# Sending the first three stores of a softmax kernel from a second queue while its loads run

## The chip, the cores and the metric

One NeuronCore of a Trainium2 chip (trn2) runs the whole kernel. The metric is the device time of one execution in microseconds (us), lower is better.

## The reference

```python
def reference(x):                      # x: 16 x 1024 x 512, float32
    x_scaled = x / 2.0
    x_max = np.max(x_scaled, axis=-1, keepdims=True)
    exp_x = np.exp(x_scaled - x_max)
    return (exp_x / np.sum(exp_x, axis=-1, keepdims=True)).astype(np.float32)
```

33.55 MB come in and 33.55 MB go out. Seen by the 128 partitions of on-chip memory there are 128 "rows" of 512 numbers per partition; one row over all partitions is 256 KB.

## The kernel before

Nine tiles of 3, 5, 9, 15, 21, 31, 15, 17 and 12 rows share one arena of 99 rows. Tiles 7 and 8 reuse the space of tiles 0 to 2 and of tile 3, so their loads wait for those tiles' stores. Compute goes by chunks of 3 to 8 rows: VectorE takes the negated maximum, ScalarE the exponentials with their sums, VectorE (two chunks later) the reciprocal and the multiply, in place.

All loads and stores are issued by SyncE on one queue, in a fixed order:

```python
PLAN = [   # per tile: rows of each chunk, first arena row
    ([3], 0), ([5], 3), ([5, 4], 8), ([5] * 3, 17), ([7] * 3, 32), ([8, 8, 8, 7], 53),
    ([5] * 3, 84), ([6, 6, 5], 0), ([4] * 3, 17),
]
QUEUE = [
    ("load", 0), ("load", 1), ("load", 2), ("load", 3), ("load", 4), ("load", 5),
    ("load", 6), ("store", 0), ("store", 1), ("store", 2), ("store", 3), ("load", 7),
    ("store", 4), ("load", 8), ("store", 5), ("store", 6), ("store", 7), ("store", 8),
]
# ... cut ...
    def do_queue(items):
        for kind, t, *rest in items:
            # ... cut ...
            if kind == "load":
                for u in behind.get(t, []):          # tiles whose space this one takes
                    nc.sync.wait_ge(st[u], stored[u])
                # ... nc.sync.dma_start(...).then_inc(ld[t], 16)
                continue
            nc.sync.wait_ge(s_mul, k + 1)            # k: last chunk of the tile
            # ... nc.sync.dma_start(...)
# ... cut ...
        for k in range(len(chunks) + LAG):           # VectorE, LAG = 2
            if k < len(chunks):
                do_max(k)
            if k >= LAG:
                do_mul(k - LAG)
```

The softmax here doesn't subtract the row's maximum and nothing guards it: scores larger than these inputs give would overflow.

## Time and profile before

| | |
|---|---|
| time, median of the first 3 runs | 163.24 us (162.96 to 163.44) |
| span of the profiled run | 161.1 us |
| VectorE busy | 125.1 us (78%) |
| ScalarE busy | 94.0 us (58%) |
| DMA packets' time, share of 16 DMA engines | 97.8% |

A row of digits on the page is the span in 40 slices of about 4 us, each digit the busy share in tenths. A queue line gives packets, MB, and the packets' time as a share of the span of all 16 DMA engines. A line of DMA issues gives the size in KB and the us from issue to landing. "SPq" is SyncE's sequencer, "ACTq" ScalarE's. In the list of waits the numbers are us in total, times, and the longest.

### The profile page before, as it was taken

The numbers are of one execution on the slowest core, as the hardware profiler recorded it, in microseconds if no ns is written. First come the engines' busy times: TensorE is split into PE (matmuls) and PEld (weight loads), VectorE is DVE, ScalarE is ACT, GpSimd is POOL, SyncE is SP. The second block draws the span as 40 slices with busy tenths as digits, with TensorE's granted clock in tenths as the row PEclk, the third lists the DMA queues.
The fourth block names the chain that finished last, engine by engine and source line by source line (L and its number), as shares of the span: only waits on it lengthen the run. The fifth ranks groups of instructions, "written<-read, shape, count | busy, mean of one in ns | idle before, by whom it ended". The sixth has DMA issues, their size and how long they took to land.

```text
span 161.1 us, 494 instructions
## 1 busy us (share of the span) xinstructions
DVE 125.1 (78%) x174; ACT 94.0 (58%) x257; POOL 0.2 (0%) x4
## 2 busy tenths in 40 slices
DVE  0557989999999999999999999999999994000000
ACT  3455957674977949696977764697875770000000
POOL 0000000000000000000000000000000000000000
DMA  7999999997996998999999989899899979999991
GB/s 264 458 476 397 458 404 480 450 490 331 504 473 286 458 397 292 458 433 458 419 413 458 480 382 491 363 416 552 349 457 489 426 340 458 409 439 415 420 464 61
DMA packets 2595, 67.13 MB, mean 417 GB/s; under 512 B 288, under 2 KB 288, under 8 KB 544
## 3 DMA queue, kind: packets, MB, share of 16 engines
q1 hardware_dynamic: 2592, 67.11, 97.8%
q14 instruction: 3, 0.02, 0.0%
HBM read 33.55 MB, written 33.55 MB: 416 GB/s over the span
## 4 chain that ended last, share of the span: by engine, by line
DVE 69%; DMA 13%; issue 0%; DVEq 0%; SPq 0%
DVE negmax L115 38%; DVE arena L128 30%; DMA arena<-in_x_dram 13%; DVE recip L124 1%; DVEq L209 0%; SPq L100 0%
## 5 line engine op out<-in xcount | busy, mean ns | idle before, releaser
L141 ACT ACTIVATE arena<-arena,negmax 128x512 f32<-128x512 f32 x128 | 90.7, 709 | 37.1 <-DVE negmax L115 37.1
L115 DVE TENSOR_REDUCE negmax<-arena 128x5 f32<-128x2560 f32 (+5 forms) x23 | 71.7, 3116 | 9.0 <-DMA arena<-in_x_dram 9.0
L128 DVE TENSOR_SCALAR arena<-arena,recip 128x512 f32<-128x512 f32 x128 | 52.8, 482 | 0.8
L141 ACT ACTIVATION_READ_ACCUMULATOR arena<-arena,negmax 128x1 f32 x128 | 23.9, 187 | 0.0
L124 DVE RECIPROCAL recip<-sums 128x5 f32<-128x5 f32 (+5 forms) x23 | 4.2, 181 | 0.0
L141 ACT ACT_TABLE_LOAD x1 | 1.3, 1283 | 1.3 <-PEq L198 1.3
L198 POOL MEMSET const-bfloat16-1.0<- 128x1 bf16 x1 | 0.1, 101 | 0.0
L198 POOL MEMSET const-uint8-127<- 128x1 uint8 x1 | 0.1, 101 | 0.0
L198 POOL MEMSET const-float32-0.0<- 128x1 f32 x1 | 0.1, 98 | 0.2 <-issue 0.2
L198 POOL MEMSET const-float32-1.0<- 128x1 f32 x1 | 0.1, 98 | 0.0
## 6 DMA issues: line engine op xcount, KB each, us to landing
arena<-in_x_dram SPq DMA_DIRECT2D x1, 7936.0 KB, 50.9
out_dram<-arena SPq DMA_DIRECT2D x1, 7936.0 KB, 36.5
arena<-in_x_dram SPq DMA_DIRECT2D x2, 3840.0 KB, 40.8
out_dram<-arena SPq DMA_DIRECT2D x2, 3840.0 KB, 32.5
arena<-in_x_dram SPq DMA_DIRECT2D x1, 5376.0 KB, 32.4
out_dram<-arena SPq DMA_DIRECT2D x1, 5376.0 KB, 32.0
arena<-in_x_dram SPq DMA_DIRECT2D x1, 4352.0 KB, 19.7
out_dram<-arena SPq DMA_DIRECT2D x1, 4352.0 KB, 25.5
```

The costliest lines, as they stand in the source:

```text
L115: nc.vector.reduce_max(out=negmax[:, b : b + c], in_=arena[:, a : a + c], axis=mybir.AxisListType.X, negate=True,)._wait_ge(ld[t], loads_o ...
L124: nc.vector.reciprocal(out=recip[:, b : b + c], in_=sums[:, b : b + c])._wait_ge(s_exp, k + 1).then_inc(s_rec, 1)
L128: ins = nc.vector.tensor_scalar_mul(out=arena[:, a + r], in0=arena[:, a + r], scalar1=recip[:, b + r : b + r + 1],)
L141: ins = nc.scalar.activation(out=arena[:, a + r], in_=arena[:, a + r], func=mybir.ActivationFunctionType.Exp, bias=negmax[:, b + r : b + r ...
L198: nc = _bacc.Bacc("TRN2", target_bir_lowering=False, num_devices=1)
```

## The change

In the kernel before, the stores of tiles 0 to 2 are ready at 17 to 32 us, but stand behind seven loads and land at 66 to 75 us. The change issues these 17 rows from ScalarE's own queue as soon as they are ready, so that they leave while the loads run and the space for tile 7 comes free early. The core of the diff:

```diff
 QUEUE = [
     ("load", 0), ("load", 1), ("load", 2), ("load", 3), ("load", 4), ("load", 5),
-    ("load", 6), ("store", 0), ("store", 1), ("store", 2), ("store", 3), ("load", 7),
+    ("load", 6), ("store", 3), ("load", 7),
     ("store", 4), ("load", 8), ("store", 5), ("store", 6), ("store", 7), ("store", 8),
 ]
+SIDE = {2: 0, 3: 1, 5: 2}          # after the exponentials of chunk k: store this tile
@@ the store part of do_queue becomes a function of the engine @@
+    def do_store(engine, t, lo, hi, groups):
+        ...
+        engine.wait_ge(s_mul, k + 1)
+        ... engine.dma_start(...)
@@ ScalarE's loop over the chunks @@
             ins.then_inc(s_exp, 1)
+            if k in SIDE:
+                do_store(nc.scalar, SIDE[k], 0, tiles[SIDE[k]][1], [(0, P, 1)])
```

## The prediction

> **What bounds the kernel now**
>
> I read the busy rows first, then the DMA part, then the chain, then the stores one by one. The page's busy rows and its queue line:
>
> ```profile
> DVE  0557989999999999999999999999999994000000
> ACT  3455957674977949696977764697875770000000
> DMA  7999999997996998999999989899899979999991
> ...
> q1 hardware_dynamic: 2592, 67.11, 97.8%
> ```
>
> Each digit is a fortieth of the span, about 4 us. VectorE has six empty slices at the end, ScalarE too; the DMA row is full from the second slice to the last but one, and the one queue's packets fill 97.8% of the 16 DMA engines' time. So the span is that of moving 67.11 MB, and 2.2% of 161.1 us, 3.5 us, is all that better packing of the same packets could ever give back. The stretches say what the ends cost:
>
> ```profile
> 0.00:2.00 2.00, 0.00 (x0) 0.74 (x1) 0.20 (x4) 1.00 0.49 117
> 60.00:64.00 4.00, 4.00 (x8) 4.00 (x12) 0.00 (x0) 1.00 0.80 250
> 66.00:84.00 18.00, 17.89 (x27) 13.82 (x39) 0.00 (x0) 1.00 1.03 444
> 158.00:161.00 3.00, 0.00 (x0) 0.00 (x0) 0.00 (x0) 1.00 0.06 25
> ```
>
> The last two columns are the DMA share and GB/s (a packet is booked where it starts, so short windows scatter around 1.00). The fill costs 1.0 us (half of 2), the closing stretch 1 to 2, and one dip at 60 to 64 us about 1.4. The change adds no byte and touches none of the three.
>
> The chain of waits would mislead here:
>
> ```profile
> DVE 69%; DMA 13%; issue 0%; DVEq 0%; SPq 0%
> ```
>
> It ends with VectorE's last multiply at 134.86 us; the 25 us of stores after that are not in it.[...]
>
> The queue in order of time, from SyncE's timeline in narrow windows (start, issue time), and the two ends of the DMA list (KB, us to landing):
>
> ```profile
> 17.31 0.35 SPq L108 DMA_DIRECT2D out_dram<-arena  x1
> 21.70 0.34 SPq L108 DMA_DIRECT2D out_dram<-arena  x1
> 31.76 0.33 SPq L108 DMA_DIRECT2D out_dram<-arena  x1
> ...
> 127.31 0.33 SPq L108 DMA_DIRECT2D out_dram<-arena  x1
> 134.89 0.33 SPq L108 DMA_DIRECT2D out_dram<-arena  x1
> ```
>
> ```profile
> out_dram<-arena SPq DMA_DIRECT2D x1, 2304.0 KB, 43.1
> out_dram<-arena SPq DMA_DIRECT2D x1, 1280.0 KB, 47.7
> out_dram<-arena SPq DMA_DIRECT2D x1, 768.0 KB, 49.0
> ```
>
> The stores of tiles 0, 1 and 2 (3, 5 and 9 rows per partition) are issued at 17.3, 21.7 and 31.8 us but land at 66.3, 69.4 and 74.9: they stand behind the seven loads issued in the first 3.9 us. That is the wait which the change removes. But the DMA engines are not idle meanwhile; they move the loads.
>
> **Rates.** The fifth load (21 rows) lands at 34.8 us and the sixth (31 rows) at 53.8: 19.0/31 = 0.613 us per row of 256 KB. The store of tile 3 (15 rows) lands at 83.95, after the one before at 74.9: 9.05/15 = 0.603 us. Loads alone and stores alone run at one rate, 428 to 435 GB/s. The 256 rows moved (128 in, 128 out) at 0.607 are 155.4 us; with 1.0 of fill, 1.4 of dip and 2 to 3 of ending that is the span.
>
> **What the Trainium skill says**
>
> "DMA: Bandwidth & Descriptors", section "Issuing engines are not separate DMA queues": transfers begun by ScalarE, SyncE or GpSimd run on the same 16 DMA engines and interleave; a second issuer saves only sequencer time. The trace of before has one queue and cannot test that; but it shows that sequencer time is not short (0.33 us per issue, 18 issues).
>
> The same page, section "Queues, rings and completion order": each DMA engine takes turns between the queue rows that have work, a packet at a time. The profile counts 2592 packets, 18 transfers of 144, and 288 of them under 512 B: so 128 data packets and 16 small ones per transfer, one data packet per partition, as long as the tile's rows (6 KB for 3 rows, 62 KB for 31). If turns are taken by these packets, a short store gets a small share beside a long load. No trace here shows it yet.
>
> The same page, section "Where 436 GB/s comes from": 435.2 GB/s for the ports of one core. The trace agrees in size: 428 to 435 on long transfers, 417 over the span. So there is no faster rate to go to, unless a load and a store in one DMA engine overlap.
>
> **The change, part by part**
>
> Removed from SyncE: three waits and three issues, 3 x 0.34 us, beside nothing that is short of time. Worth 0.
>
> Added on ScalarE: after the exponentials of chunks 2, 3 and 5, a wait and an issue of about 0.35 us (up to 0.8, as the longest on SyncE). The waits are for the multiplies of chunks 0, 1 and 3, done at 17.3, 21.7 and 31.7 us; the three exponential groups end at 19.5, 22.4 and 33.6. So ScalarE waits little or not at all. In ScalarE's timeline it then idles for the next maximum: 2.59 us before the exponential at 25.03 and 0.89 before that at 34.49. The second and third issues fall into this, and the first pushes the next five exponentials by 0.4 us, which the 2.59 swallow. On the path: 0.
>
> Moved: 17 rows of store, 17 x 0.61 = 10.4 us of DMA time, from after the seventh load to between the loads. The loads after it land later by at most 10.4 us. What that does on VectorE: the fourth load is used as it lands (a 0.50 us wait before the maximum at 22.18); the fifth lands at 34.8 and is used at 36.57, 1.7 to spare; the sixth lands at 53.8 and is used at 55.37, 1.5 to spare; the seventh lands at 64.4 and is used at 84.97, 20 to spare. If turns are by packet, the sixth load has the 3- and 5-row stores and part of the 9-row one ahead of it, 6 to 7 us, and VectorE falls back by 4 to 5 us in all; if bytes are shared evenly, by up to 10.4 - 1.5 = 8.9 us. So I expect new waits of VectorE for loads, 13 to 18 us instead of 9.0, and its last multiply at 139 to 144 us instead of 134.9.
>
> Does that reach the end? Only if the store queue runs dry. From issue to landing, less the own time at 0.61 us per row, the later stores queue for: tile 5, 36.5 - 18.9 = 17.6 us; tile 6, 29.8 - 9.2 = 20.6; tile 7, 25.5 - 10.4 = 15.1; tile 8, 25.2 - 7.3 = 17.9. The least is 15.1 us, above the greatest delay of 8.9. The eighth load waits for the stores of tiles 0 to 2, now done some us sooner; it stands behind the store of tile 3 anyway, and that store and the seven loads and 17 rows before it end at about 84 us in either order. The ninth load waits for that same store. From there both kernels do the same work in the same order.
>
> Sum: 0 (SyncE) + 0 (ScalarE) + 0 (the same 256 rows at the same rate) = no change. I add 0.1 us for the second queue's upkeep, a guess: 163.3 us.
>
> **The rivals**
>
> A: a load and a store in flight together overlap within a DMA engine, as one reads main memory while the other reads on-chip memory. For it: each direction alone sits at the same ceiling, which leaves open that the two are separate. Against it: where loads and stores meet in one queue (66 to 84 us ends in a load behind a store) nothing runs above 445 GB/s over a stretch long enough to trust. If 17 rows were fully hidden, 10.4 us go, to 153; half of it, 158.
>
> B: mixing reads and writes costs rate, in the memory or at each switch between queues. Against it: the switches within one queue leave no gap. Over some 55 us of mixed traffic, 3% would be 1.6 us: 165.
>
> C: VectorE, made late by the loads, becomes the bound. It has 15.1 us to spare against 8.9; it would need a delay nearly twice what I work out. If it were 17 us late, 165.
>
> D: the dip at 60 to 64 us (1.4 us) is chance of that run and moves or goes: 162 or so, in either kernel.
>
> **Range and chances**
>
> The three runs of before spread over 0.5 us. D allows about 1 us down, B 1 to 1.5 up: 162.2 to 164.6 in 8 of 10. Faster by over 2% means under 160.0, which is below the sum of packets, fill and ending, so only A does it: 0.05. Slower by over 2%, over 166.5, needs a strong B, or C: 0.05. Within 2%: 0.90.
>
> **What would show each step right or wrong**
>
> Right: a queue line for ScalarE's queue with 4.46 MB and one for SyncE's with the rest, together 97 to 98%; the three early stores landing before 74.9 us; more than 9.0 us of VectorE waiting for loads, the longest new waits before the maxima of tiles 4 and 5; VectorE's empty slices at the end fewer by one or two; the last landing unmoved. Packet turns: the 3-row store taking about 10 us to land though it is 1.8 us of work. Wrong: GB/s above 450 held between 20 and 60 us (A); a combined share above 98% with a longer span (B); empty digits in the DMA row after 84 us (C).

## The result and the profile after

The first measurement gave 162.77 us (median of 4 runs, 162.50 to 162.99) against 163.10 us (4 runs) for the kernel before: ratio 0.9976, 95% interval 0.9952 to 1.0001. A ratio is the mean time of one kernel's fast runs over that of the other's of the same rounds, so it is not quite the ratio of the medians. Executions over 1.5% slower than the fastest of the same kernel are left out of the means. The outputs are correct. Within 2%, as predicted, and inside the range.

The busy rows and the queue lines of the changed kernel's page:

```profile
DVE  0557979998999909999999999999999999800000
...
DMA  7999999999798969999999999899899979999991
...
q1 hardware_dynamic: 2160, 62.65, 91.3%
q10 hardware_dynamic: 432, 4.46, 6.5%
```

Two queues now, 91.3% and 6.5%: together the same 97.8% as before. VectorE has one empty slice fewer at the end and a hole at about 56 to 60 us, with the DMA row still full under it. So work was moved and none was saved.

The rate was not the same everywhere, though. Two stretches, first of the kernel before, then of the changed one (the last column is GB/s):

```profile
40.00:60.00 20.00, 19.86 (x26) 15.34 (x43) 0.00 (x0) 1.00 1.00 425
60.00:64.00 4.00, 4.00 (x8) 4.00 (x12) 0.00 (x0) 1.00 0.80 250
```

```profile
40.00:60.00 20.00, 16.44 (x23) 15.14 (x42) 0.00 (x0) 1.00 0.96 402
60.00:64.00 4.00, 3.34 (x1) 0.00 (x0) 0.00 (x0) 1.00 0.96 415
```

The dip at 60 to 64 us is gone, and the stretch before it, where the load of tile 5 now runs beside a store, is slower. The packet records size both. In the kernel before, the packets of load 6 took 1.29 us on the mean, in the changed one 1.14: with eight packets per DMA engine, 1.2 us less. The packets of loads 3, 4 and 5 went from 1.14, 1.59 and 2.35 us to 1.16, 1.62 and 2.44: 1.1 us more in all. The two nearly cancel.

The three stores in ScalarE's timeline (start, issue time), and their lines among the DMA issues:

```profile
17.32 0.38 ACTq L100 DMA_DIRECT2D out_dram<-arena  x1
...
21.72 0.34 ACTq L100 DMA_DIRECT2D out_dram<-arena  x1
...
32.22 0.34 ACTq L100 DMA_DIRECT2D out_dram<-arena  x1
```

```profile
out_dram<-arena ACTq DMA_DIRECT2D x1, 768.0 KB, 19.0
...
out_dram<-arena ACTq DMA_DIRECT2D x1, 1280.0 KB, 38.3
...
out_dram<-arena ACTq DMA_DIRECT2D x1, 2304.0 KB, 42.3
```

They land at 36.3, 60.0 and 74.6 us, against 66.3, 69.4 and 74.9 before. The one that the load of tile 7 waits for, the last, gained 0.3 us. The stretch from 23 to 32 us says why; these are its two queues:

```profile
q1 hardware_dynamic: 79, 3.40, 87.2%
q10 hardware_dynamic: 80, 0.49, 13.0%
```

In 9 us, 79 packets of the load of tile 4 and 80 packets of the store of tile 0: one for one. The load's packets are 42 KB and the store's 6 KB, so equal turns give the store one eighth of the bytes. Each of the 16 DMA engines has eight data packets of every transfer; store 0 passes load 4, store 1 passes load 5, and store 2 passes load 6, which ends at 74.4 us itself.

VectorE's waits for loads, first in the kernel before, then in the changed one:

```profile
DVE negmax L115 <- DMA arena<-in_x_dram: 9.0, 4, 4.5
```

```profile
DVE negmax L122 <- DMA arena<-in_x_dram: 14.1, 6, 4.5
```

Two new waits. The longer stands in the changed kernel's chain of waits under a label of its own, and the next piece is VectorE's maximum:

```profile
56.55 4.09 another core or an unknown queue
60.64 0.02 issue
60.66 4.42 DVE negmax L122
```

There is no other core here: the load of tile 5 lands at 60.6 us (2.9 + 57.7), where it landed at 53.8. A name in the chain is a guess of the profile; the landing settles it. VectorE's last multiply ends at 140.2 us, 5.3 later than before, and the last store still lands at 160 us.

### The profile page after: what moved, and what is told of

It is laid out like the page before. It is cut to its first block, busy times and chain, and to the rows that moved or that the text cites. A ratio compares the mean times of both kernels' runs of the same rounds, so it can differ in the third digit from the quotient of the medians.

```text
span 160.9 us, 494 instructions
## 1 busy us (share of the span) xinstructions
DVE 125.2 (78%) x174; ACT 94.0 (58%) x257; POOL 0.2 (0%) x4
## 3 DMA queue, kind: packets, MB, share of 16 engines
q1 hardware_dynamic: 2160, 62.65, 91.3%
## 4 chain that ended last, share of the span: by engine, by line
DVE 61%; DMA 22%; another core or an unknown queue 3%; SPq 1%; issue 0%; DVEq 0%
DVE negmax L122 33%; DVE arena L135 27%; DMA arena<-in_x_dram 22%; DVE recip L131 1%; SPq L115 1%; DVEq L218 0%
## 5 line engine op out<-in xcount | busy, mean ns | idle before, releaser
L122 DVE TENSOR_REDUCE negmax<-arena 128x5 f32<-128x2560 f32 (+5 forms) x23 | 71.7, 3116 | 14.1 <-DMA arena<-in_x_dram 14.1
## 6 DMA issues: line engine op xcount, KB each, us to landing
arena<-in_x_dram SPq DMA_DIRECT2D x1, 7936.0 KB, 57.7
```

Source lines behind the costliest of these rows:

```text
L122: nc.vector.reduce_max(out=negmax[:, b : b + c], in_=arena[:, a : a + c], axis=mybir.AxisListType.X, negate=True,)._wait_ge(ld[t], loads_o ...
```

## The experiments

The first eight runs test the account "the bytes set the end, turns by packet set the landings, VectorE pays out of spare time". The last four follow up something seen on the way. Each kernel was run beside the kernel before on the same chip. The rivals are an overlap of loads and stores within a DMA engine, costs of switching, and VectorE as the bound.

### The changed kernel again

No edit.

> The changed kernel once more, in five rounds, to settle whether the 0.24% it gained in the first runs is there. Theory bytes (the 16 DMA engines move the same 256 rows at the same rate, so order and queue do not matter): ratio to before 0.997 to 1.000, 162.6 to 163.2 us. Theory overlap (a load and a store share a DMA engine at some profit): ratio clearly below 0.998 in every round. In the profile, as in the first: stores of tiles 0, 1, 2 landing at about 36, 60 and 74.5 us.

Measured: 163.22 us (6 runs) against 163.36 (11 runs), ratio 0.9997 (0.9982 to 1.0012). The stores land at 36.3, 59.7 and 74.2 us. The first set's 0.24% is not a gain that one can count on; the change is neutral.

### The order alone, on one queue

```diff
 # the kernel before
-("load", 4), ("load", 5), ("load", 6), ("store", 0), ("store", 1), ("store", 2), ("store", 3), ...
+("load", 4), ("store", 0), ("store", 1), ("load", 5), ("store", 2), ("load", 6), ("store", 3), ...
```

> The kernel before with the order alone changed, all on SyncE's one queue: stores 0 and 1 put between loads 4 and 5, store 2 between loads 5 and 6. Theory bytes: the same time as before within 0.4%. In a single queue whole transfers follow each other, so store 0 lands at about 37, store 1 at about 40, load 5 at 58 to 59, store 2 at about 64, load 6 at about 74; VectorE waits about 3.5 us before the first maximum of tile 5 and its last multiply ends at about 138 us. Theory overlap (the gain needs two queues at once): this one stays at before's time while the changed kernel is below it.

Measured: 164.28 us, ratio 1.0050 (1.0028 to 1.0072), a little outside what was expected. In one queue whole transfers do follow each other: stores 0 and 1 land at 38.4 and 41.4 us, not at 36 and 60. Load 5 lands at 61.3, store 2 at 66.7, load 6 at 76.2, all 1.4 to 2.8 us later than worked out, and VectorE's last multiply ends at 140.8 us (138 expected). The page's GB/s row shows one loss:

```profile
GB/s 279 440 474 385 468 490 370 456 205 581 359 405 501 421 329 453 419 445 415 438 439 445 456 399 456 391 439 508 433 390 437 499 318 453 441 427 428 424 356 18
```

The ninth slice, 33 to 37 us, has 205 GB/s: the dip that the kernel before has at 60 to 64 us. In the trace's packet records it is the last packets of the load just ahead of the first store (some two per DMA engine), most of them 0.2 to 1.4 us too long: load 6 in the kernel before, load 4 here. So the dip is no chance of one run; it went where the first store went. Why it arises is open. And order is not quite indifferent: as a plain order on one queue this one is 0.5% worse. Its packets took 157.9 us per DMA engine against 157.6, and its slowest DMA engine ended later (table below); why is open.

### All stores on ScalarE's queue

```diff
-SIDE = {2: 0, 3: 1, 5: 2}
+SIDE = {2: 0, 3: 1, 5: 2, 8: 3, 11: 4, 15: 5, 18: 6, 21: 7, 22: 8}
 # and no stores left in SyncE's QUEUE
```

> The changed kernel with all nine stores on ScalarE's queue, so that loads and stores share the DMA engines up to the last load, about twice as many rows mixed. Theory bytes: 162.3 to 163.3 us. Theory overlap: 0.5% or more below the changed kernel. Theory switching costs: above the changed kernel by 0.5% or more. By turns, load 7 (with store 3 beside it) lands at about 94 us and load 8 (issued at about 93, after store 3, with store 4 beside it) at about 113, both as before.

Measured: 162.17 us (162.06 to 162.24), ratio 0.9925 (0.9911 to 0.9940): 1.2 us under the kernel before, 1.0 under the changed kernel in the same rounds. That is what the overlap theory asked for, so its packets have to be looked at:

```profile
q1 hardware_dynamic: 1296, 33.56, 49.6%
q10 hardware_dynamic: 1296, 33.56, 48.5%
```

98.1% of a span of 160.4 us is 157.4 us of packets per DMA engine; 97.8% of the changed kernel's 160.9 is 157.4 as well. The packets did not get fewer, are hardly shorter, and do not lie on top of each other: what shrank is mainly the rest of the span. Loads 7 and 8 landed at 99.8 and 122.8 us, not at 94 and 113 as I expected (load 7 was still passing store 4, whose packets are longer than store 3's). Where the 1.2 us come from is taken up below.

### One long load cut in two

```diff
-("load", 5),
+("load", 5, 0, 16, [(0, 128, 1)]), ("load", 5, 16, 31, [(0, 128, 1)]),
```

> The changed kernel with load 5 (31 rows) issued as two transfers of 16 and 15 rows; nothing else. Theory turns by packet (each DMA engine takes one packet of each queue in turn, a packet being one partition's rows of one transfer): store 1's eight packets per engine go past the eight packets of the first half, 8 x (1.21 + 0.385) = 12.8 us from 36 us, so it lands at about 49 to 50 us instead of 60; store 2 passes the second half and lands at about 64.5 instead of 74.5; load 5 is then later, at about 64 instead of 60.7, and VectorE waits about 7.5 us for it instead of 4.1. Theory turns by bytes or by time (an even share): the size of a load's packets is indifferent, store 1 lands at about 60 as in the changed kernel. In both the total is 162.4 to 163.3 us, as VectorE's spare is not used up.

Two lines of this kernel's DMA issues, for stores 1 and 2:

```profile
out_dram<-arena ACTq DMA_DIRECT2D x1, 1280.0 KB, 27.9
...
out_dram<-arena ACTq DMA_DIRECT2D x1, 2304.0 KB, 31.9
```

Issued at 21.7 and 32.3 us, they land at 49.6 and 64.2 us, as turns by packet have it (49 to 50 and 64.5); an even share of bytes or time would have left store 1 at 60. Load 5 lands at 64.9 us, VectorE waits 8.2 us for it (7.5 expected), and its last multiply ends at 144.5 us. Yet the time is 162.74 us, ratio 0.9963 (0.9949 to 0.9978). Another 4 us of lateness on VectorE cost nothing.

### Without the three early stores

```diff
-            if k in SIDE:
-                do_store(nc.scalar, SIDE[k], 0, tiles[SIDE[k]][1], [(0, P, 1)])
 # the load of tile 7 waits for the multiplies of tiles 0 to 2 in place of their stores
```

The result is wrong: 17 rows stay unwritten.

> The changed kernel without the three early stores (17 of 128 rows per partition stay unwritten: wrong on purpose). Theory bytes: 17 x 0.61 = 10.4 us less, 152.0 to 153.0 us; VectorE's last multiply back at about 134.9 us. Theory hidden (stores beside loads are partly free): less is saved, so 154 us or more.

```profile
q1 hardware_dynamic: 2160, 62.65, 97.2%
...
HBM read 33.55 MB, written 29.10 MB: 414 GB/s over the span
```

Measured: 152.99 us against 163.23. The 17 rows are worth 10.24 us, 0.602 us each: the full price of a row. Nothing of these stores was hidden beside the loads in the changed kernel; they were paid for at the rate at which they are paid for anywhere. VectorE's last multiply ended at 134.7 us, as expected.

### VectorE made late on purpose

```diff
+            if k == 14:             # ahead of tile 6; n maxima whose results nobody uses
+                for i in range(n):
+                    nc.vector.reduce_max(out=spare[...], in_=<chunk 14>, ...)
             if k < len(chunks):
                 do_max(k)
```

Three runs: the changed kernel with n = 3 (8.2 us), the changed kernel with n = 6 (16.4 us), the kernel before with n = 6.

> The changed kernel with three more maxima of 5 rows on VectorE (2.73 us each, 8.2 us together, result unused) before the first maximum of tile 6. Theory spare (VectorE can be late as long as the DMA queue has stores left; in the changed kernel store 7 is issued at 132.6 us and its first packet starts at 140.0 on the fastest and about 142 on the slowest DMA engine): the last multiply ends 8.2 us later, at about 148, and the time moves by 0 to 0.4 us. Theory VectorE bound: 8.2 us more, 171 us.

> The same with six more maxima, 16.4 us. Theory spare: store 5 is issued at about 118.7 and could have started at 112 to 114, so the queue runs dry for about 5.4 us; store 7 is issued at about 149 and makes it dry for some 2.6 us more: 170.5 to 171 us, some 8 us over the changed kernel and not 16.4. Theory VectorE bound: 179 us.

> The kernel before with the same six more maxima, 16.4 us. Its VectorE runs about 5 us ahead of the changed kernel's, so theory spare: store 5, at about 113.3, is just in time, store 7, at about 143.7, leaves the queue dry for some 2.6 us: 165.5 to 166.2 us. So the same lateness that costs the changed kernel 8 us costs this one under 3: what the change spends is spare of VectorE, not time. If the change had spent no spare, both would lose the same.

| kernel | VectorE added | last multiply ends | time | over 163.23 us |
|---|---|---|---|---|
| changed | 8.2 us | 148.2 us | 163.18 us | 0.0 |
| changed | 16.4 us | 156.6 us | 170.88 us | 7.7 |
| before | 16.4 us | 151.2 us | 165.59 us | 2.4 |

VectorE eight microseconds later and not a tenth more of time: it is not the bound. At 16.4 us the spare is used up. The changed kernel's added maxima in VectorE's timeline, and the DMA row of the stretch from 105 to 120 us in the same run (40 slices of 0.375 us):

```profile
90.30 16.44 DVE L168 TENSOR_REDUCE spare<-arena 128x5 f32<-128x2560 f32 x6
```

```profile
DMA  9797999979799797996303000000000000000090
```

The DMA engines have nothing to do from about 113 to 119 us: the store queue ran dry, as expected in place and size. The two kernels' costs for the same lateness differ by 7.7 - 2.4 = 5.3 us, which is just what VectorE had fallen back by in the changed kernel (140.2 - 134.9). So the change did cost something after all: spare, not time.

### The all-ScalarE version once more, and what part of it gains

```diff
 # the late stores on ScalarE, the early three behind the loads on SyncE
-SIDE = {2: 0, 3: 1, 5: 2}
+SIDE = {8: 3, 11: 4, 15: 5, 18: 6, 21: 7, 22: 8}
 # the third run: all stores on ScalarE, and load 5 cut in two as above
```

> All nine stores on ScalarE's queue once more, to see whether its 0.75% is there in another set of runs, and to stand beside the next two on one chip. If it is: ratio to before 0.991 to 0.995, the last store landing 1.5 to 2 us after the first of the 16 DMA engines is done with it. If it was chance: 0.997 to 1.000.

> The early three stores back on SyncE behind the seven loads as before, the six later ones on ScalarE. It tells which part of the all-ScalarE version's 1.2 us is whose. Theory late sharing (the DMA engines drift apart by 2 to 3 us, and loads 7 and 8 sharing them with stores evens that out): this one has the whole gain, ratio 0.991 to 0.995. Theory early sharing (the move of the three stores is what gains, the rest spends it): ratio 0.998 to 1.002.

> All stores on ScalarE and load 5 in two transfers of 16 and 15 rows, the two edits that came out below the kernel before, together. If their gains add: ratio 0.988 to 0.991 (161.4 to 161.9 us). If both are the same evening out of the DMA engines: 0.991 to 0.995. Bytes say it cannot be under 160 us in either case.

The repetition: 161.98 us against 163.37, ratio 0.9922 (0.9903 to 0.9942). The gain is there.

The late stores alone: 172.32 us, ratio 1.0544. My expectation was wrong altogether, and the profile says how. First the page's busy rows, then VectorE's and SyncE's waits:

```profile
DVE  0649989999999799999999991000079999999000
...
DMA  7999989989994999999998698998997799069994
```

```profile
DVE negmax L121 <- DMA arena<-in_x_dram: 31.9, 6, 22.0
```

```profile
SPq L112 <- DMA out_dram<-arena: 64.4, 1, 64.4
```

SyncE waits 64.4 us for the early stores. These now stand behind the loads in SyncE's queue while stores 3 and 4, with packets of 30 and 42 KB, take turns with that queue from ScalarE's. Load 7 goes out at 96.5 us in place of 75, VectorE is without data for 22.0 us, and later the DMA engines have gaps (the 7 7 and 0 6 in their row). The same two queues as in the best version, with the wrong stores in the second one, cost 9 us. The spare accounts for it: VectorE's last multiply ends at 158.0 us, 23.1 later than in the kernel before, and the late runs above showed 14.0 of that to be free. As a test of the 1.2 us it settles nothing.

With load 5 cut in two as well: the fast runs are 162.29 to 163.37 us, ratio 0.9969 (0.9945 to 0.9993); two of six runs were slow (167.1 and 167.5 us). The two small gains do not add: neither expected range was met, and the cut load made the all-ScalarE version slower (161.98 us in the same rounds).

### Stores 0 to 4 on ScalarE, the last four on SyncE

```diff
-SIDE = {2: 0, 3: 1, 5: 2}
+SIDE = {2: 0, 3: 1, 5: 2, 8: 3, 11: 4}
 # stores 3 and 4 leave SyncE's QUEUE, stores 5 to 8 stay in it behind load 8
```

> The changed kernel with stores 3 and 4 on ScalarE as well (those that run beside loads 7 and 8), stores 5 to 8 back on SyncE, where no load is left beside them. Theory late sharing (what the all-ScalarE version gains comes from loads 7 and 8 sharing the DMA engines with stores, so that the slowest DMA engine ends nearer to the mean): ratio to before 0.991 to 0.995, and loads 7 and 8 land at about 98 to 100 and 120 to 123 us as there. Theory last stores (it comes from the queue that the last four stores are in): ratio 0.998 to 1.001.

Measured: 162.28 us (161.87 to 163.42, 6 runs), ratio 0.9947 (0.9908 to 0.9986). Load 7 lands at 100.0 us as expected, load 8 at 114.0 and not at 120 to 123: store 5 now waits behind it instead of running beside it. One run in six sits at 163.4, so the interval is wide and just reaches 0.998; and seven of the eight runs of the kernel before are those of the earlier set on this chip. It leans to the sharing beside loads 7 and 8 over the queue of the last four stores, no more.

Where this gain lies can be read from the records of the trace: the last store's completion is counted up in 16 steps, each 0.3 to 0.5 us after one of its 16 small closing packets, which I take as one for each DMA engine. In us from the span's start:

```
kernel                          first   mean    last
before                          158.0   158.6   160.1
changed                         157.9   158.6   159.9
changed, again                  157.9   158.6   160.4
order alone, one queue          158.3   159.1   161.8
one long load cut in two        157.8   158.4   160.2
all on ScalarE                  157.7   158.4   159.3
all on ScalarE, again           157.7   158.4   159.2
stores 0 to 4 on ScalarE        157.7   158.3   159.4
all on ScalarE, load 5 cut      157.7   158.4   160.0
```

The mean hardly moves; the slowest DMA engine does, and it sets the end. That the sharing evens the engines out is argued, not shown, and the last row speaks against it: there loads 7 and 8 share with stores too, and the slowest engine ends at 160.0 us. Each row is one profiled run; which engine lags, and why, no run tells. The best version, all stores on ScalarE, beats the kernel before by 0.7 to 0.8% in two sets and the changed kernel by 0.6% in one, below the 2% that I call a difference, but clear of noise against the kernel before.

## Why the prediction was right

- **Bytes set the end.** Right. The queue shares add up to the same 97.8%, dropping 17 rows gave back 10.24 us where 10.4 were worked out, and VectorE 8.2 us later cost nothing. That the sum came out at zero to a few tenths was in part luck: it took the dip as untouched and mixing as free, and instead the dip's 1.2 us per DMA engine went and 1.1 us of longer load packets came.
- **SyncE 0, ScalarE 0.** Right: issues of 0.34 to 0.38 us, ScalarE busy for 94.0 us in both. A detail was off: the issues come at 17.3, 21.7 and 32.2 us, not after the exponentials ahead of them (19.5, 22.4, 33.6), since ScalarE's sequencer ran ahead of its engine. (ScalarE's row also has seven empty slices at the end, not six.)
- **VectorE's delay.** Right for turns by packet: last multiply at 140.2 us (139 to 144 was said), 5.3 us later where turns by packet were to give 4 to 5, 14.1 us of waits (13 to 18), load 5 later by 6.8 us (6 to 7).
- **VectorE's spare of 15.1 us.** Right in kind, some 1 us too large: 16.4 us of lateness cost the kernel before 2.4 us, so 14.0 of them were free.
- **Store 0 lands in about 10 us.** Mis-sized: it took 19.0. Eight store packets must pass eight packets of 42 KB, 8 x (1.59 + 0.23) = 14.6 us, and the first of them started 3.8 us after its issue, in the packet records, as load 3's packets were finished first. I had not multiplied out the turns. So tile 7's space came free at 74.6 us, hardly sooner than before; it did not matter, as the load of tile 7 stands behind store 3 anyway.
- **Rival A, overlap:** refuted by the dropped stores. **B, cost of mixing:** not ruled out, and small: the load packets beside the early stores took 1.1 us per DMA engine longer in all. It is no fixed rate, as loads 7 and 8 beside stores in the all-ScalarE version took their usual 1.29 and 0.91 us a packet, and that version is the fastest. **C, VectorE as the bound:** refuted, and located at 8 to 9 us more of delay. **D, the dip as chance:** wrong; in every single-queue kernel that was profiled it stands just ahead of the first store. The prediction held against B that switches within one queue leave no gap, and the dip lies at just such a switch. It cost the forecast nothing, as the changed kernel loses about as much in small pieces between 18 and 58 us. Whether that is the same loss in another place, no run tells.

## What to carry to other kernels

When the DMA engines are full and no compute engine runs out of spare, moving a transfer to another queue or another place changed landings and spare, and the time by under 1% here: count bytes first, then ask who can still be starved. Two queues took turns by packet here, so a transfer with short packets beside one with long packets lands late, however small it is; cut the long one if the short one matters. And put the stores that free space for loads where nothing with long packets can get ahead of them: the late-stores version lost 9 us that way.

## What the Trainium skill lacked or had wrong

- "DMA: Bandwidth & Descriptors", section "Queues, rings and completion order", gives packets of typically 9 to 17 descriptors as the unit of a turn. Here the turn was one record of the profile, one partition's whole run: 79 against 80 packets in 9 us, of 42 and 6 KB. How many descriptors such a record holds, the profile does not say. With eight such per DMA engine and transfer, two transfers in two queues go in lockstep, and a store of 1.8 us of work took 19.0 us; the page does not draw that consequence.
- The same section does not say how far a queue has committed itself when a second one gets work: the first store's first packet came 3.8 us after its issue, about three load packets of 1.14 us.
- The same page, section "Issuing engines are not separate DMA queues", says that a second issuer only saves issue time. For the bytes this agrees (97.8% in both kernels, 10.24 us for 17 rows). But the choice of queue alone moved the time between 162.0 and 172.3 us, through landings and waits, and that is missing.
- The same page, section "Latency and other measured facts", calls two of the 16 DMA engines usually slower, gives no size, and guesses at a cause in DMAs issued from GpSimd. Missing is a size for the drift under plain loads and stores from SyncE and ScalarE: 1.5 to 3.5 us between the first DMA engine and the last at the end of 160 us.
- No page that I read has the dip in the last load packets ahead of the first store: 205 to 261 GB/s over some 4 us, and the load's packets 1.2 to 1.5 us per DMA engine longer in all, in each of the four single-queue kernels profiled.
